# An encoder layer's MLP beginning in another order, finishing work in steps of 512 columns, and four side steps per block in the last gate group

## The chip, the cores and the metric

The kernel runs on one core of one Trainium2 chip. The metric is the device time of one execution in microseconds (us). Each time given for a kernel is the median of several runs; the profile is of one execution, taken by the hardware profiler. The engines are TensorE (PE, matrix products; PEld is its loading of weights), VectorE (DVE), ScalarE (ACT), GpSimd (POOL) and SyncE (SP), which here issues the DMA transfers.

## The reference

One layer of an encoder on 1536 tokens of width 1024 (512 tokens of one request and 1024 of another), in float32:

```python
def _layer(h, p_i, ...):
    a = _rmsnorm(h, norm_mix_g)
    z = a @ w_in                                   # q, k, v, and the pooling channels u
    o_attn = _attention(q, k, v, q_norm_g, k_norm_g)
    o_pool = _pool_mixer(u, w_pool, pool_scale)
    h = h + jnp.concatenate([o_attn, o_pool], axis=-1) @ w_out
    m = _rmsnorm(h, norm_mlp_g)
    h = h + jnp.square(jax.nn.relu(m @ w_up)) @ w_down       # hidden width 4096
    gate = jax.nn.sigmoid(_rmsnorm(h, norm_ple_g) @ w_ple_gate)
    h = h + gate * (p_i @ w_ple_proj)
    return h
# and a last _rmsnorm(h, final_norm_g)
```

## The kernel before

**Layout and chunks.** Everything is kept transposed: the 1024 features lie on partitions, tokens are columns. The tokens are three chunks c = 0, 1, 2 of 512 columns; the residual h of a chunk is four tiles `hT[c][a]` of 128 x 2 x 512 (256 features each, two halves of 512 columns in a row; 512 KB). Each float32 product is made of three products of a high and a low half (`three`): the high half is a cast by ACT to a shorter format, the low half the difference, made by POOL or DVE.

**Stages, by the trace:** the input projection to about 194 us, attention and the pooling mixer with the output projection (`heads_out`, which adds into h) to 579, the MLP to 1613, and the gate and the last norm to the end.

**The MLP** runs over 48 `Pair`s: 16 for each chunk, each of two blocks of 128 of the 4096 hidden units. A pair makes the hidden values by seven products in Strassen's manner, in the order 1, 6, 2, 5, 7, 3, 4, into four banks (x, y, z, q; tiles px, py, pz, pq). Its weights `w..._i` are sums of the loaded `wur` (L793 to L804, DVE), cast by ACT (L786) and with a low half by POOL (L787). The factors on the other side, `mo`, are the seven combinations of the normalised h; `make_m(c)` computes them chunk by chunk in advance, stores them to DRAM (L636) and has them loaded again. It also computes w, the mean square of h (the norm's factor), as `acc[:, 1]` (tile sqm), and stores it to `w_d` (L647). The pair ends in a chain: DVE adds bank q (L870 for product 7, L880 for product 4), ACT makes relu and two squares (L875 to L877 and L881 to L883), DVE the low half of r (L886). The next pair's products are mixed with `down(a)` of this one: 12 products of r and the down weights wd, added to h by DVE (L837). The order on TensorE is px(1), `down(0)`, py(6), px(2), `down(1)`, pz(5), pq(7), `down(2)`, pz(3), pq(4), `down(3)`.

The norm's factor is not applied to m. Instead h is multiplied by w before the MLP's sums are added to it (`raise_h`, L662, eight steps on DVE), and at the chunk's end by its inverse (`invert`, L670, and L1138).

**Side work.** After each of the seven products the loop calls `after(i)`: one step of `feeding` (the weights of pairs ahead; the next `load_up()` is issued in its step 3), one step of `splits` (the down weights, L816, L817), one of `raising`, and `step()`, one step of a list of generators called `chores`: `spill`, `invert`, `make_m`, and `finishing(c)`, which in the MLP of chunk c + 1 scales the finished h of chunk c, stores it to `hl_d`, squares it on ACT (L1142) and for c = 0 makes the gate's input (L1126). Chores run one behind another, so a longer one delays those behind it.

**What sets the order.** PE, ACT, DVE and POOL run their instructions in the order in which the program issues them; SP's transfers are put in order by a scheduler, and each waits for the eighth before it on the ring of semaphores. Buffers come from 49 slots in turn (`slot`): a new tile takes the slot of an old one and waits for the last reader of it, which can be a DMA that stores the old tile.

The last part is `gate`, called for (c, o, w) = (0, 0, 512), (1, 0, 512), (2, 0, 256), (2, 256, 256); each has eight blocks d of 24 matmuls (tile pg), and `hooks` lists the k at which a chore's step is taken in a block.

## Time and profile before

| | before |
|---|---|
| median of 3 runs | 1814.47 us (1813.41 to 1815.92) |
| profiled execution | 1813.31 us, span 1811.5 |
| PE busy | 1759.7 us, 97% |
| DVE busy | 1260.0 us, 70% |
| ACT busy | 939.7 us, 52% |
| POOL busy | 1053.7 us, 58% |
| DMA | 256.84 MB, mean 142 GB/s |

Rows of a timeline give the start, the duration, the engine, the line, the operation, the tile written and those read, and the count of instructions in the row; in square brackets how long the engine stood idle before it and what released it. "PE pd L49 <- DVE r L886: 10.6, 11, 1.8" in a list of waits says that PE, at its product into pd, waited for DVE's r of line 886 10.6 us in all, 11 times, at most 1.8 us. "issue" stands where the profile shows no release. SPq is the queue from which SP issues transfers. Line 49 is the helper of all matrix products, line 56 that of all loads. Numbers of chunks and pairs are left out of the names of tiles in the profile.

### The profile page before, as it was taken

To read this page: it belongs to the slowest core of one execution; us is meant where nothing else is said; L and a number is where in the kernel's file an instruction comes from. 1 tells how busy PE (TensorE), PEld (TensorE's weight loads), DVE (VectorE), ACT (ScalarE), POOL (GpSimd) and SP (SyncE) were. 2 spreads that over 40 slices of the span, in tenths; PEclk is the share of its full clock that TensorE was granted. 3 is DMA by queue.
4 is the path that set the end of the run, shared out by engine and by line. 5 is a ranking of instruction groups with operands and counts; after the bars stand their busy time and mean duration, and the time that the engine had idled before them with its cause. 6 is when DMAs were issued, how large, how long until landed. Compare 5 with 4: busy or idle time off the path is not lost.

```text
span 1811.5 us, 28604 instructions
## 1 busy us (share of the span) xinstructions
PE 1759.7 (97%) x10540; PEld 1537.1 (85%) x10540; DVE 1260.0 (70%) x1843; ACT 939.7 (52%) x1854; POOL 1053.7 (58%) x923
## 2 busy tenths in 40 slices
PE   9999899999999799999999999999999999999997
PEld 7888777888868798988888889889898999888887
DVE  5677865888894677865568877876776556665655
ACT  6434455768794455655445545554455444443332
POOL 3474774535674567676656776785577666543121
PEclk9999999999999899999999999999999999999998
DMA  6333545120519335343364442556443323272102
GB/s 248 114 123 105 216 165 185 36 94 13 206 46 367 139 122 198 121 177 100 136 265 157 163 151 96 195 185 235 179 157 100 110 94 99 89 262 70 59 12 82
DMA packets 83883, 256.84 MB, mean 142 GB/s; under 512 B 9888, under 2 KB 16416, under 8 KB 83744
## 3 DMA queue, kind: packets, MB, share of 16 engines
q1 hardware_dynamic: 83744, 255.02, 39.7%
q8 instruction: 83, 1.36, 0.3%
q14 instruction: 56, 0.46, 0.1%
HBM read 195.74 MB, written 59.24 MB: 141 GB/s over the span
## 4 chain that ended last, share of the span: by engine, by line
PE 78%; DVE 7%; ACT 5%; DMA 3%; issue 3%; POOL 1%; POOLq 0%; DVEq 0%; ACTq 0%; SPq 0%
PE pd L49 25%; PE z L49 7%; PE px L49 6%; PE pz L49 6%; PE pq L49 6%; PE pg L49 6%; PE py L49 4%; PE pp L49 3%; PE o L49 3%; PE tp L53 3%; PE po L49 3%; PE S L49 3%; PE pj L49 1%; DMA wur<-in_w_up_dram 1%; DVE r L886 1%
## 5 line engine op out<-in xcount | busy, mean ns | idle before, releaser
L49 PE MATMUL pd<-r,wd 128*128 128x512 f32 x2304 | 568.5, 395 | 10.8 <-DVE r L886 10.6
L49 PEld LDWEIGHTS pd<-r,wd 128*128 128x128 f32 x2304 | 419.5, 188 | 100.3 <-DVE r L886 16.1
L787 POOL TENSOR_TENSOR w<-ws,w 128x512 fp32r<-128x512 f32 x192 | 272.5, 1423 | 217.9 <-ACT w L786 206.8
L787 POOL TENSOR_TENSOR w<-wur,w 128x512 fp32r<-128x512 f32 x144 | 212.8, 1489 | 135.4 <-ACT w L786 134.4
L837 DVE TENSOR_TENSOR h<-pd,h 128x1024 f32<-128x1024 f32 x192 | 233.5, 1216 | 76.6 <-PE pd L49 76.5
L786 ACT CAST w<-ws 128x512 fp32r<-128x512 f32 x192 | 118.5, 617 | 271.1 <-DVE ws L795 241.1
L461 POOL TENSOR_SCALAR pr<-pr,rr 128x512 f32<-128x512 f32 x160 | 111.2, 705 | 134.7 <-DVE rr L456 66.8
L49 PE MATMUL z<-w,x 128*128 128x512 f32 (+1 forms) x864 | 175.7, 359 | 0.9 <-DVE w L160 0.5
L49 PEld LDWEIGHTS pz<-mo,w 128*128 128x128 f32 x1152 | 150.7, 190 | 19.3 <-issue 11.2
L49 PEld LDWEIGHTS z<-w,x 128*128 128x128 f32 x864 | 142.9, 189 | 28.0 <-ACT w L159 2.1
L49 PE MATMUL pz<-mo,w 128*128 128x256 f32 x1152 | 153.6, 283 | 10.2 <-issue 10.2
L817 DVE TENSOR_TENSOR wd<-wdr,wd 128x512 fp32r<-128x512 f32 x96 | 102.8, 1071 | 83.1 <-ACT wd L816 76.6
L49 PE MATMUL pq<-mo,w 128*128 128x256 f32 x1152 | 153.7, 283 | 1.0 <-issue 1.0
L49 PE MATMUL px<-mo,w 128*128 128x256 f32 x1152 | 152.2, 281 | 0.0
L49 PEld LDWEIGHTS px<-mo,w 128*128 128x128 f32 x1152 | 146.5, 189 | 4.0
L49 PEld LDWEIGHTS pq<-mo,w 128*128 128x128 f32 x1152 | 144.7, 191 | 1.4 <-issue 1.3
L49 PE MATMUL pg<-hg,wg 128*128 128x512 f32 (+1 forms) x768 | 141.0, 338 | 0.2
L472 ACT CAST pt<-tp 128x512 fp32r<-128x512 f32 x160 | 88.0, 591 | 88.5 <-PE tp L53 86.8
L49 PEld LDWEIGHTS pg<-hg,wg 128*128 128x128 f32 x768 | 118.6, 188 | 17.8 <-DVE hg L1128 1.0
L817 POOL TENSOR_TENSOR wd<-wdr,wd 128x512 fp32r<-128x512 f32 x96 | 131.8, 1373 | 2.6 <-DMA w_d<-sqm 2.6
L886 DVE TENSOR_TENSOR r<-c,r 128x512 fp32r<-128x512 f32 x96 | 74.7, 783 | 74.1 <-ACT c L883 46.2
L473 DVE TENSOR_TENSOR pt<-tp,pt 128x512 fp32r<-128x512 f32 x160 | 104.0, 684 | 31.4 <-ACT pt L472 31.1
(195 smaller groups left out, 3036.2 us busy)
## 6 DMA issues: line engine op xcount, KB each, us to landing
wur<-in_w_up_dram SPq DMA_DIRECT2D x96, 512.0 KB, 4.2
wdr<-in_w_down_dram SPq DMA_DIRECT2D x96, 512.0 KB, 4.4
mo_d<-mm SPq DMA_DIRECT2D x84, 256.0 KB, 2.3
mo<-mo_d SPq DMA_DIRECT2D x42, 512.0 KB, 7.7
h_d<-h SPq DMA_DIRECT2D x16, 512.0 KB, 3.0
h<-h_d SPq DMA_DIRECT2D x16, 512.0 KB, 9.9
xn<-in_xn_dram SPq DMA_DIRECT2D x12, 512.0 KB, 6.4
qs_d<-qs SPq DMA_DIRECT2D x12, 512.0 KB, 3.0
```

Of the source, the lines that this page charges most:

```text
L49: last_pe[0] = nc.tensor.matmul(*a, **k).ins
L53: last_pe[0] = nc.tensor.transpose(*a, **k).ins
L461: gp.tensor_scalar(p, p, rr, 1.0, op0=ALU.mult, op1=ALU.mult)
L472: sc.copy(self.pt[kt][:, 0], tp)
L473: ve.tensor_tensor(self.pt[kt][:, 1], tp, as32(self.pt[kt][:, 0]), op=ALU.subtract)
L786: sc.copy(t[:, 0], x)
L787: gp.tensor_tensor(t[:, 1], x, as32(t[:, 0]), op=ALU.subtract)
L817: (gp, ve)[i].tensor_tensor(lo, self.dr[i][:, h], as32(hi), op=ALU.subtract)
L837: ve.tensor_tensor(h, pd.rearrange("p (a b) -> p a b", a=2), h, op=ALU.add)
L886: ve.tensor_tensor(self.r[i][:, 1], x, as32(self.r[i][:, 0]), op=ALU.subtract)
```

## The change

- `make_m(0)` keeps w of chunk 0 in its tile (`ws[0] = acc[:, 1]`): it isn't stored to `w_d` and loaded again; `load_ms` is called for chunks 1 and 2 alone.
- The h of chunk 2 is stored to `h_d` right in `heads_out`, tile by tile at odd d, where before `spill(2)` did it after 16 steps of waiting. The chores behind it (`invert(0)`, `make_m(1)`) are then the next in the list.
- The loads of pair 1's up weights are issued ahead of those of h of chunk 0, not in `feeding`'s step 3 of pair 0.
- Ahead of the MLP five steps of `feeding` are taken instead of four; in pair 0 no step of it follows product 4, `splits` runs after products 5, 7, 3 and 4 alone, and `raise_h` takes two steps after 2, 5, 7 and 3 (none after 1 and 6). From pair 1 on the steps stand as before.
- `finishing` squares a tile in halves of 512 columns with a step for each, and makes the two halves of the gate's input in two steps: 38 steps for chunk 0 instead of 26, 22 for chunk 1 instead of 18.
- In the gate groups with o > 0, the last one, `hooks` are (1, 3, 6) in every block: with the `step()` ahead of the block four steps, where there were two.

```diff
@@ -644,7 +644,10 @@
         for i in range(2):
             pe.matmul(bc, ones_sb, sh[:, i], start=i == 0, stop=i == 1)
         ve.tensor_scalar(acc[:, 1], bc, 1.0 / D, EPS, op0=ALU.mult, op1=ALU.add)
-        sy.dma_start(w_d[c], acc[:, 1])
+        if c:
+            sy.dma_start(w_d[c], acc[:, 1])
+        else:
+            ws[0] = acc[:, 1]
 
     def load_mo(c, i):
         MO[c, i] = [slot([P, 4, HF], F32R, f"mo{c}_{i}{j}") for j in range(2)]
@@ -703,7 +706,6 @@
     away = set()
 
     def spill(c):
-        yield from wait(16 if c == 2 else 0)
         for a in range(4):
             sy.dma_start(h_d[c][a], hT[c][a])
         away.add(c)
@@ -753,7 +755,10 @@
                     for i, (w_, x_) in enumerate(three(ws, [x[:, k, :] for x in cat[p]])):
                         pe.matmul(po, w_, x_, start=k == 0 and i == 0, stop=k == 3 and i == 2)
                 ve.tensor_tensor(h, po, h, op=ALU.add)
-                if d == KD - 1 and p % 2:
+                if p == 5:
+                    if d % 2:
+                        sy.dma_start(h_d[c][d // 2], hT[c][d // 2])
+                elif d == KD - 1 and p % 2:
                     chores.append(spill(c))
                     if c == 0:
                         chores.append(make_m(0, gp, gp))
@@ -893,7 +898,7 @@
 
         for n, pr in enumerate(pairs):
             for i, _ in enumerate(pr.feed()):
-                if i == 3 and n + 1 < len(pairs):
+                if i == 3 and 0 < n < len(pairs) - 1:
                     pairs[n + 1].load_up()
                 yield
     feeding = stream()
@@ -1067,12 +1072,13 @@
 
     pairs[0].load_down()
     load_mo(0, ORDER[5]), load_mo(0, ORDER[6])
+    pairs[1].load_up()
     for a in range(4):
         load_h(0, a, h_d[0][a])
     while fill:
         fill.popleft()()
         step(2)
-        if len(fill) % 2 == 0 and len(fill) < 8:
+        if len(fill) % 2 == 0 and len(fill) < 12:
             next(feeding)
     ps_free()
     acc_free()
@@ -1139,10 +1145,12 @@
                 yield
             sy.dma_start(hl_d[c][a], h)
             sq = slot([P, 2, CH], F32, f"sqg{c}{a}") if a else acc
-            sc.activation(sq, h, AF.Square)
-            if c == 0:
-                gate_in(0, a, True)
-            yield
+            for e in range(2):
+                sc.activation(sq[:, e], h[:, e], AF.Square)
+                yield
+            for e in range(2) if c == 0 else ():
+                gate_in(0, a, True, (e,))
+                yield
             for e in range(2) if a else ():
                 gp.tensor_tensor(acc[:, e], acc[:, e], sq[:, e], op=ALU.add)
                 yield
@@ -1184,7 +1192,7 @@
             if c:
                 for a in range(4):
                     load_h(c, a, h_d[c][a])
-            load_ms(c)
+                load_ms(c)
             raising = raise_h(c)
         if g == 1:
             chores.append(invert(c))
@@ -1202,9 +1210,11 @@
                 pairs[n + 1].load_down()
 
         def after(i):
-            next(feeding, None)
-            next(splits, None)
-            if raising:
+            if n or i != 4:
+                next(feeding, None)
+            if n or i in (5, 7, 3, 4):
+                next(splits, None)
+            for _ in range(0 if not raising else 1 if c else 0 if i in (1, 6) else 2):
                 next(raising, None)
             if g == NG - 1 and c < 2:
                 load_mo(c + 1, i)
@@ -1244,7 +1254,7 @@
                 pe.matmul(pj, w_, x_, start=k == 0 and i == 0, stop=k == 1 and i == 2)
         step()
         pg = ps("g", f"pg{c}{o}{d}")[:, :w]
-        hooks = () if c == 1 and d == KD - 1 or c == 2 and o == 0 else (2, 5) if c == 1 else (3,)
+        hooks = (1, 3, 6) if o else () if c == 1 and d == KD - 1 or c == 2 and o == 0 else (2, 5) if c == 1 else (3,)
         if c == 0 and d % 2 == 0 and d < KD - 2:
             for j in range(2):
                 load_g(d // 2 + 1, j)
```

SP's transfers at the MLP's beginning, before (h00 to h03 are chunk 0's tiles, h20 to h23 chunk 2's, wur0_10 and wur0_11 the up weights of pair 1, h_d2 the spilled h of chunk 2):

```order
L56 DMA mo0_41_6354<-mo_d0_41_275 128x1024
L56 DMA h00_6357<-h_d0_0_304 128x1024
L56 DMA h01_6359<-h_d0_1_305 128x1024
L56 DMA h02_6361<-h_d0_2_306 128x1024
L56 DMA h03_6363<-h_d0_3_307 128x1024
L647 DMA w_d0_259<-sqm0_4189 128x512
L708 DMA h_d2_0_312<-h20_5526 128x1024
L708 DMA h_d2_1_313<-h21_5528 128x1024
L708 DMA h_d2_2_314<-h22_5530 128x1024
L56 DMA wur0_10_6531<-in_w_up_dram 128x1024
L56 DMA wur0_11_6532<-in_w_up_dram 128x1024
L56 DMA w0_6556<-w_d0_259 128x512
```

and now:

```order
L56 DMA mo0_41_6354<-mo_d0_41_275 128x1024
L56 DMA wur0_10_6357<-in_w_up_dram 128x1024
L56 DMA wur0_11_6358<-in_w_up_dram 128x1024
L56 DMA h00_6361<-h_d0_0_304 128x1024
L56 DMA h01_6363<-h_d0_1_305 128x1024
L56 DMA h02_6365<-h_d0_2_306 128x1024
L56 DMA h03_6367<-h_d0_3_307 128x1024
L760 DMA h_d2_0_312<-h20_5526 128x1024
L760 DMA h_d2_1_313<-h21_5528 128x1024
L760 DMA h_d2_2_314<-h22_5530 128x1024
L760 DMA h_d2_3_315<-h23_5532 128x1024
L56 DMA wdr0_10_6622<-in_w_down_dram 128x1024
```

The store and load of w are gone, the up weights stand ahead of h, and all four spills of chunk 2's h stand together behind the loads of h.

DVE's row in pair 0, from the add of product 5 on, before (c0_0 is the pair's hidden values, r0_00 and r0_01 its result, wd0 its down weights):

```order
L866 TENSOR_TENSOR u0_0_6558<-pz0_0_6630,u0_0_6558 128x256
L793 TENSOR_TENSOR ws0_10_6644<-wur0_11_6532 128x512
L817 TENSOR_TENSOR wd0_011_6583<-wdr0_01_6346,wd0_010_6582 128x512
L662 TENSOR_TENSOR h01_6359<-h01_6359,w0_6556 128x512
L870 TENSOR_TENSOR c0_0_6559<-pq0_0_6653,u0_0_6558 128x256
L795 TENSOR_TENSOR ws0_10_6644<-ws0_10_6644,wur0_10_6531 128x512
L662 TENSOR_TENSOR h02_6361<-h02_6361,w0_6556 128x512
L874 TENSOR_TENSOR c0_0_6559<-pz0_0_6630,u0_0_6558 128x256
L662 TENSOR_TENSOR h02_6361<-h02_6361,w0_6556 128x512
L880 TENSOR_TENSOR c0_0_6559<-pq0_0_6653,u0_0_6558 128x256
L801 TENSOR_TENSOR ws0_11_6645<-wur0_10_6531,wur0_11_6532 128x512
L662 TENSOR_TENSOR h03_6363<-h03_6363,w0_6556 128x512
```

and now:

```order
L871 TENSOR_TENSOR u0_0_6563<-pz0_0_6626,u0_0_6563 128x256
L800 TENSOR_TENSOR ws0_10_6614<-ws0_10_6614,wur0_10_6357 128x512
L665 TENSOR_TENSOR h01_6363<-h01_6363,sqm0_4189 128x512 x2
L875 TENSOR_TENSOR c0_0_6564<-pq0_0_6652,u0_0_6563 128x256
L665 TENSOR_TENSOR h02_6365<-h02_6365,sqm0_4189 128x512 x2
L879 TENSOR_TENSOR c0_0_6564<-pz0_0_6626,u0_0_6563 128x256
L806 TENSOR_TENSOR ws0_11_6615<-wur0_10_6357,wur0_11_6358 128x512
L822 TENSOR_TENSOR wd0_011_6647<-wdr0_01_6346,wd0_010_6646 128x512
L665 TENSOR_TENSOR h03_6367<-h03_6367,sqm0_4189 128x512 x2
L885 TENSOR_TENSOR c0_0_6564<-pq0_0_6652,u0_0_6563 128x256
L822 TENSOR_TENSOR wd0_011_6647<-wdr0_01_6346,wd0_010_6646 128x512
L891 TENSOR_TENSOR r0_00_6565<-c0_0_6564,r0_00_6565 128x512
```

The multiplications of h (L662, now L665) come in twos, and both differences of the down weights (L817, now L822) stand between product 3's add and r. The tile c0_0 now takes the slot of h20 and the weight w0_1_1 of pair 1 that of h21, so L875 on DVE and L866 on ACT wait for the store of h20, and the cast of w0_1_1 (L791) on ACT for that of h21. In ACT's row the casts of pair 0's down weights moved with them, before:

```order
L786 CAST w0_0_3_6601<-ws0_01_6431 128x512
L816 CAST wd0_000_6580<-wdr0_00_6345 128x512
L861 ACTIVATE c0_0_6559<-px0_0_6562 128x256
L786 CAST w0_0_4_6620<-wur0_01_6098 128x512
L816 CAST wd0_010_6582<-wdr0_01_6346 128x512
L786 CAST w0_1_1_6646<-wur0_10_6531 128x512
L816 CAST wd0_010_6582<-wdr0_01_6346 128x512
L786 CAST w0_1_6_6668<-ws0_10_6644 128x512
L875 ACTIVATE c0_0_6559<-c0_0_6559 128x256
L876 ACTIVATE r0_00_6560<-c0_0_6559 128x512
L877 ACTIVATE c0_0_6559<-c0_0_6559 128x512
L786 CAST w0_1_2_6688<-wur0_10_6531 128x512
```

and now:

```order
L791 CAST w0_1_1_6616<-wur0_10_6357 128x512
L791 CAST w0_1_6_6641<-ws0_10_6614 128x512
L821 CAST wd0_000_6644<-wdr0_00_6345 128x512
L791 CAST w0_1_2_6666<-wur0_10_6357 128x512
L821 CAST wd0_000_6644<-wdr0_00_6345 128x512
L880 ACTIVATE c0_0_6564<-c0_0_6564 128x256
L881 ACTIVATE r0_00_6565<-c0_0_6564 128x512
L882 ACTIVATE c0_0_6564<-c0_0_6564 128x512
L791 CAST w0_1_5_6689<-ws0_10_6614 128x512
L821 CAST wd0_010_6646<-wdr0_01_6346 128x512
L886 ACTIVATE c0_0_6564<-c0_0_6564 128x512
L887 ACTIVATE r0_01_6566<-c0_0_6564 128x512
```

The second block's casts (wd0_010) now stand on either side of r0_01's chain.

ACT's row in chunk 1, at the work on chunk 0's tile h01 (sqg01 its squares, hg01 the gate's input), before:

```order
L786 CAST w1_3_1_10605<-wur1_30_10461 128x512
L816 CAST wd1_210_10511<-wdr1_21_10360 128x512
L786 CAST w1_3_6_10627<-ws1_30_10603 128x512
L1142 ACTIVATE sqg01_10631<-h01_6359 128x1024
L1126 ACTIVATE hg01_0_10633<-h01_6359,gple_sb_230 128x512 x2
L875 ACTIVATE c1_2_10488<-c1_2_10488 128x256
L876 ACTIVATE r1_20_10489<-c1_2_10488 128x512
L877 ACTIVATE c1_2_10488<-c1_2_10488 128x512
```

and now:

```order
L1149 ACTIVATE sqg01_10730<-h01_6363 128x512
L791 CAST w1_3_3_10760<-ws1_31_10597 128x512
L821 CAST wd1_300_10723<-wdr1_30_10578 128x512
L1149 ACTIVATE sqg01_10730<-h01_6363 128x512
L866 ACTIVATE c1_3_10702<-px1_3_10705 128x256
L791 CAST w1_3_4_10779<-wur1_31_10459 128x512
L821 CAST wd1_310_10725<-wdr1_31_10579 128x512
L1132 ACTIVATE hg01_0_10784<-h01_6363,gple_sb_230 128x512
L791 CAST w1_4_1_10821<-wur1_40_10680 128x512
L821 CAST wd1_310_10725<-wdr1_31_10579 128x512
L1132 ACTIVATE hg01_0_10784<-h01_6363,gple_sb_230 128x512
L791 CAST w1_4_6_10843<-ws1_40_10819 128x512
```

The square of 1024 columns and both halves of the gate's input stood in a row ahead of a relu (L875); now single halves stand apart, with casts between them.

SP's row at the change from chunk 1 to chunk 2, now (w_d2 is chunk 2's w; before, the store stood 19 rows ahead of wur2_10, right behind wur1_151):

```order
L56 DMA mo2_31_13599<-mo_d2_31_301 128x1024
L648 DMA w_d2_261<-sqm2_11936 128x512
L56 DMA wur2_10_13627<-in_w_up_dram 128x1024
L56 DMA wur2_11_13628<-in_w_up_dram 128x1024
L56 DMA mo2_40_13631<-mo_d2_40_302 128x1024
L56 DMA mo2_41_13632<-mo_d2_41_303 128x1024
L56 DMA h20_13651<-h_d2_0_312 128x1024
L56 DMA h21_13653<-h_d2_1_313 128x1024
L56 DMA h22_13655<-h_d2_2_314 128x1024
L56 DMA h23_13657<-h_d2_3_315 128x1024
L56 DMA w2_13659<-w_d2_261 128x512
```

The 256 KB store stands ahead of the up weights of pair 1 and of the load of h and w.

## The prediction

> **What bounds the kernel now.** I read the page first, then TensorE's waits, then the stretches where those waits lie, engine by engine. The page gives TensorE (PE) nearly the whole span:

> ```profile
> span 1811.5 us, 28604 instructions
> PE 1759.7 (97%) x10540; PEld 1537.1 (85%) x10540; DVE 1260.0 (70%) x1843; ACT 939.7 (52%) x1854; POOL 1053.7 (58%) x923
> ```

> So only PE's idle time (1811.5 - 1759.7 = 51.8 us) and its half-clock time can be won; a step saved on another engine counts where PE waits for it. TensorE's waits name two kinds:

> ```profile
> PE pd L49 <- DVE r L886: 10.6, 11, 1.8
> PE pz L49 <- issue: 10.2, 3, 9.2
> ```

> In the first `down` waits for the low half of r, the last product of a pair's chain ACT, ACT, ACT, DVE; in the second one wait of 9.2 us has no releaser named. TensorE's timeline puts that one at the MLP's beginning:

> ```profile
> 583.28 1.59 PE L49 MATMUL pz<-mo,w 128*128 128x256 f32 x12
> 584.71 1.57 PE L49 MATMUL pq<-mo,w 128*128 128x256 f32 x12
> 595.48 2.90 PE L49 MATMUL pz<-mo,w 128*128 128x256 f32 x12 [9.20 <-issue]
> ...
> 602.18 0.40 PE L49 MATMUL pd<-r,wd 128*128 128x512 f32 x1
> 604.34 0.96 PE L49 MATMUL pd<-r,wd 128*128 128x512 f32 x3 [1.77 <-DVE r L886]
> 607.99 1.60 PE L49 MATMUL py<-mo,w 128*128 128x256 f32 x12
> ```

> DVE's timeline tells why. Product 3 adds into bank z, which L866 must have read; L866 stands behind h's multiplication, which waited for w to come back from DRAM:

> ```profile
> 592.22 0.69 DVE L662 TENSOR_TENSOR h<-h,w 128x512 f32<-128x512 f32 x1 [11.38 <-DMA w<-w_d]
> ...
> 594.96 0.42 DVE L866 TENSOR_TENSOR u<-pz,u 128x256 f32<-128x256 f32 x1
> ...
> 601.91 1.77 DVE L662 TENSOR_TENSOR h<-h,w 128x512 f32<-128x512 f32 x1
> 603.61 2.38 DVE L886 TENSOR_TENSOR r<-c,r 128x512 fp32r<-128x512 f32 x2
> ```

> The windows of that stretch (columns: window, length, then PE, PEld, DVE, ACT and POOL busy, granted clock, DMA share, GB/s) show full queues and afterwards a halved clock:

> ```profile
> 586.20:595.40 9.20, 0.08 (x1) 0.00 (x0) 3.18 (x7) 1.14 (x2) 5.44 (x5) 0.74 1.02 413
> 595.40:598.40 3.00, 2.92 (x14) 2.95 (x15) 3.00 (x6) 0.25 (x1) 0.00 (x0) 0.50 0.30 122
> 598.40:602.60 4.20, 4.18 (x25) 3.85 (x24) 3.90 (x6) 3.69 (x7) 2.47 (x2) 0.71 0.23 27
> ```

> At 413 GB/s a 512 KB transfer takes 524288 / 413000 = 1.27 us. After the stall two products (24 matmuls) took from 595.48 to 600.74 = 5.26 us, where an undisturbed one takes 1.43 (pz at 583.28 to pq at 584.71): 5.26 - 2.86 = 2.4 us lost to the clock.

> **The beginning, part by part.** w no longer goes through DRAM, so that wait is gone. What is late next? The transfers ahead of the new order are those of SP's rows: mo4, two wur, four h, four spilled h_d2. To place them I need one landing of before: ACT's first cast of pair 1 was released by its wur.

> ```profile
> 590.35 0.62 ACT L786 CAST w<-wur 128x512 fp32r<-128x512 f32 x1 [5.46 <-DMA wur<-in_w_up_dram]
> ...
> 599.53 0.63 ACT L876 ACTIVATE r<-c 128x512 fp32r<-128x512 f32 x1
> 600.19 0.63 ACT L877 ACTIVATE c<-c 128x512 f32<-128x512 f32 x1
> 600.73 0.60 ACT L786 CAST w<-wur 128x512 fp32r<-128x512 f32 x1
> ```

> In before's order eight and a half transfers of 512 KB (four h, the 256 KB of w_d, three h_d, this wur) lie between mo4 and that moment, so mo4 landed at about 590.3 - 8.5 x 1.27 = 579.5. In after's order the same pace gives wur 580.8 and 582.0, h 583.3 to 587.1, h_d2 tile 0 at 588.4, tile 1 at 589.6. Two of these are new waits: c of pair 0 now takes the buffer that h's tile 0 of chunk 2 left, so DVE's L875 and ACT's relu L866 wait for the spill of tile 0; the weight w of pair 1's product 1 takes tile 1's buffer, so ACT's cast L791 waits for 589.6. Behind L875 on DVE stand the whole rest of the pair's chain; behind L866 and the cast on ACT the same.

> PE then runs product 3 from 586.1 without the stall, idles from 587.5 until L875 has read bank q (588.9), runs product 4 to 590.3, idles until POOL has made the low half of the weight. POOL's timeline has its price:

> ```profile
> 591.04 1.26 POOL L787 TENSOR_TENSOR w<-wur,w 128x512 fp32r<-128x512 f32 x1 [0.67 <-ACT w L786]
> ```

> 589.6 + 0.6 + 1.3 = 591.5, so px of pair 1 ends at 592.9, and PE needs r. ACT has from 589.6: three casts of w and two of wd (pitch 0.54, by the rows above), relu, two squares (0.66, 0.54), one more cast of w and one of wd: about 5.3 us, to 595.0. Then DVE's wd difference and h's last two multiplications stand ahead of L885: 3 x 0.6 = 1.8 us alone, 3 x 1.75 = 5.2 beside POOL (1.77 against 0.69 for L662 above). Then ACT relu, two squares, a cast (2.4 us) and DVE's wd difference and first L886 (1.2 to 3): r's low half at 601.2 if DVE is never held, 604.1 if it is. In before the same mix of casts, POOL differences and h multiplications was held, so I take 603.7. From there 2.9 us of `down` and the half clock's 2.4 us (PE is idle from 592.9 for over 8 us, nearly as long as the 9.2 that halved it before) put py of pair 1 at 609.0, against 607.99: **+1.0 us**. Ends: 601.2 with no clock loss, 604.1 - 608 = -3.9; 604.1 with POOL a difference (1.3) later, +2.5.

> [...]

> [...]

> The fifth feed step is work taken from pair 0; from pair 1 on the distance is as before, so chunk 0's interior counts 0 (±0.5).

> **End of a chunk's MLP (finishing).** The time from a pair to the next is read where DVE adds q of product 4:

> ```profile
> 963.41 0.42 DVE L880 TENSOR_TENSOR c<-pq,u 128x256 f32<-128x256 f32 x1 [0.40 <-PE pq L49]
> 984.48 0.42 DVE L880 TENSOR_TENSOR c<-pq,u 128x256 f32<-128x256 f32 x1 [0.88 <-PE pq L49]
> 1006.62 0.42 DVE L880 TENSOR_TENSOR c<-pq,u 128x256 f32<-128x256 f32 x1
> 1029.69 0.42 DVE L880 TENSOR_TENSOR c<-pq,u 128x256 f32<-128x256 f32 x1
> 1052.76 0.42 DVE L880 TENSOR_TENSOR c<-pq,u 128x256 f32<-128x256 f32 x1 [0.38 <-PE pq L49]
> ```

> An undisturbed pair takes 21.07; the next three take 22.14, 23.07, 23.07: 5.07 us lost. ACT's rows in the second show the cause:

> ```profile
> 1005.73 1.05 ACT L1142 ACTIVATE sqg<-h 128x1024 f32<-128x1024 f32 x1
> 1006.69 1.32 ACT L1126 ACTIVATE hg<-h,gple_sb 128x512 fp32r<-128x512 f32 x2
> 1007.92 0.40 ACT L875 ACTIVATE c<-c 128x256 f32<-128x256 f32 x1
> ```

> 2.2 us of side work stand ahead of the relu, which could have run at 1006.6. After has a step of at most 0.6 there, spread over four; the pairs' own slack took less than 2.2 - 2.0 = 0.2 of it, so a half step (0.5) can still show in a pair: **-4.8** (ends -5.1, all of it; -3.5, 0.5 left in each of three pairs). With a step for each half the work on chunk 0's end takes twelve steps more, and chunk 2's preparation, which runs behind it in the same list, comes later. Its casts then meet relu chains in other pairs; before they cost 1.5 once:

> ```profile
> PE pd L49 <- DVE r L886: 1.5, 1, 1.5
> ```

> (TensorE's waits from 1130 to 1165.) After, by the order, one pair has two 0.7 us ACTIVATEs ahead of its relu where that pair had two casts: **-0.2**, between -1.5 (no such meeting) and +1.5 (two).

> In chunk 2 the Square stands between the fourth product's add and its relu:

> ```profile
> 1354.34 0.42 DVE L880 TENSOR_TENSOR c<-pq,u 128x256 f32<-128x256 f32 x1
> 1376.61 0.43 DVE L880 TENSOR_TENSOR c<-pq,u 128x256 f32<-128x256 f32 x1
> ...
> 1356.63 1.06 ACT L1142 ACTIVATE sqg<-h 128x1024 f32<-128x1024 f32 x1
> ```

> 22.27 - 21.07 = 1.2 lost; in halves and in other steps **-1.2** (-0.5 where one half, 0.5, still stands there; -1.4).

> **The seam from chunk 1 to 2.** The later preparation moves the 256 KB store of w into the one stretch where SP's transfers fall behind: w's load was issued at 1270.69 and landed ten us later.

> ```profile
> 1261.92 0.81 SPq L56 DMA_DIRECT2D wur<-in_w_up_dram  x2
> ...
> 1270.69 0.32 SPq L56 DMA_DIRECT2D w<-w_d  x1
> ...
> 1267.58 0.42 DVE L880 TENSOR_TENSOR c<-pq,u 128x256 f32<-128x256 f32 x1 [1.01 <-PE pq L49]
> ...
> 1280.34 1.14 DVE L662 TENSOR_TENSOR h<-h,w 128x512 f32<-128x512 f32 x1 [7.16 <-DMA w<-w_d]
> ```

> A transfer of half the size ahead makes w 0.64 later: **+0.65**, 0.3 if part of it is covered, 1.3 if the store also holds a ring's place.

> **The last gate group.** Two more steps per block empty the side work sooner, but the end follows the last block's own chain:

> ```profile
> 1799.19 0.42 DVE L1268 TENSOR_TENSOR s<-pg,bcs 128x256 f32<-128x256 f32 x1 [0.56 <-PE pg L49]
> ...
> 1801.54 0.83 PE L49 MATMUL ssf<-ones_sb,s 128*128 128x1 f32 x6 [1.16 <-ACT s L1272]
> ```

> Its first operation waits for PE, so it isn't late by side work: **0** (±0.3: PE's small sums stand earlier among its matmuls, and may wait a few tenths for POOL).

> **Sum:** +1.0 + 0 - 4.8 - 0.2 + 0.65 - 1.2 + 0 = -4.55. The profiled execution took 1813.31 (span 1811.5), so its counterpart comes to 1808.8; the median of the runs, 1814.47, lies 1.16 higher: **1810.0 us**. What a measurement can tell from no change is 0.2%, 3.6 us: the line lies at 1810.8.

> **Rivals.**
> [...]
> *C, the steps don't remove the chunk's losses.* Twice as many small pieces meet the relus in more pairs, or POOL's differences get held by DVE's more scattered work; then half or less of the 5.07 and 1.2 comes back. -2.5 and -0.3 in place of -4.8 and -1.2, with +1.0, +0.65 and +1.0 of casts: 1814.3. For it: relu chains that are late by single casts exist (the 1.5 above). Against it: pairs with a cast alone run at 21.07.
> *D, slower: the seam.* The store of w stands ahead of SP's load of wur at 1261.92 and can't leave before DVE has computed w, in after just behind the pair's last q (DVE does the row's L880 there at 1267.6). If SP stands still these 5.8 us long enough for the transfers in flight to run out, w's load lands 5.8 later, DVE's multiplication and the banks behind it too, and PE idles that long and then loses the clock's 2.4: +8.2, in all 1814.5 + 3.6 = 1818. It decides if the backlog at 1261.9 is under 5.8 us; against it speaks w's load, which took ten us to land, so a backlog of about eight.

> **How the numbers follow.** Main case 0.63 (1810.0, own range 1806 to 1813: the ends of the terms, not all at once); B 0.11; C 0.20; D 0.06. The main case lies under 1810.8 in 65 of 100, 0.41. Faster: 0.41 + 0.11 + 0.02 of C = 0.54. Same: 0.22 + 0.16 of C = 0.38. Slower: 0.06 + 0.02 of C = 0.08. The range 1805 to 1816 leaves out B and D, 0.17.

> **What would show it.** Beginning: DVE L875 released by a DMA h_d2 at about 588.5, PE's largest gap 7 to 10 us long but behind px of pair 1, a clock of 0.5 behind it, py at 606 to 610. Chunk 1: the three pairs at 21.1 to 21.6 instead of 22.1 to 23.1, TensorE's wait for r (10.6) down to about 6. Chunk 2: one pair less at 22.3. Seam: DVE's wait for w 0.6 longer. I am wrong if the pairs of chunk 1 stay above 22, or if h_d2 lands before 586 or after 591.

## The result, and the profile after

The changed kernel takes 1833.45 us (median; 1832.98 to 1836.97), before 1814.57: a ratio of 1.0108, 95% interval 1.0096 to 1.012. It is slower by 19 us, where 1810.0 was forecast. The profiled execution has a span of 1831.5 us, 20.0 more than before's 1811.5.

The page of the changed kernel, first lines, and then TensorE's longest waits in it:

```profile
span 1831.5 us, 28583 instructions
PE 1768.5 (97%) x10540; PEld 1541.7 (84%) x10540; DVE 1254.4 (68%) x1843; ACT 940.6 (51%) x1862; POOL 1049.2 (57%) x923
```

```profile
PE pd L49 <- DVE r L891: 23.2, 12, 10.0
PE pd L49 <- DVE h L842: 5.4, 1, 5.4
```

PE is idle 63.0 us instead of 51.8; its busy time grew by 8.8 with the same 10540 products, as products at a halved clock take longer: eleven products into pd took 2.69 us at 1188.68, at the clock 1.00, and 4.63 at 1194.94, with the clock at 0.50 from 1195.02 to 1198.43. The 10.2 us of before's wait at pz are gone, and the wait for r grew from 10.6 to 23.2; its longest, 10.0 us, is the beginning's.

Where the 20 us arose is read from the times at which DVE adds product 4 of a pair (the rows L880, now L885), as in the prediction. A table of the differences between such rows, from the two traces, and of the kernels run afterwards (us; "0.1" is pair 1 of chunk 0):

| stretch | before | changed | finishing only | 12 idle steps | idle steps behind the factor | b6 |
|---|---|---|---|---|---|---|
| first px to py of pair 0.1 | 28.98 | 29.49 | | | | 19.39 |
| 0.1 to 0.15 | 296.60 | 297.64 | 296.64 | 296.63 | 296.68 | 296.20 |
| 1.1 to 1.6 | 111.79 | 108.51 | 108.63 | 110.51 | 111.84 | 109.29 |
| 1.6 to 1.9 | 63.64 | 71.84 | 72.34 | 72.26 | 63.44 | 63.53 |
| 1.9 to 1.15 | 128.74 | 135.35 | 134.07 | 134.19 | 134.12 | 128.51 |
| 1.15 to 2.0 | 23.96 | 29.73 | 30.24 | 30.31 | 30.02 | 21.95 |
| 2.0 to 2.15 | 318.18 | 318.53 | 318.35 | 318.58 | 318.48 | 317.66 |

The gain of the finer steps is there (-3.3 in 1.1 to 1.6). What came on top are three losses behind it: 8.2, 6.6 and 5.8 us. Of the first two numbers, 1.3 us are one and the same work: TensorE's ten small products for the gate norm's factor (ssg, 0.81 us from its start to the next product's, and bcg, 0.46) left the stretch 1.1 to 1.6 for 1.6 to 1.9. Before, and then changed:

```profile
1060.96 0.95 PE L49 MATMUL ssg<-ones_sb,sqg 128*128 128x1 f32 x8
```

```profile
1094.41 0.95 PE L49 MATMUL ssg<-ones_sb,sqg 128*128 128x1 f32 x8
```

Without that move the gain is 2.0 us and the first loss 6.9.

**The first, pair 1.7.** DVE's timeline, and then POOL's, in the changed kernel:

```profile
1094.61 0.42 DVE L885 TENSOR_TENSOR c<-pq,u 128x256 f32<-128x256 f32 x1 [0.99 <-PE pq L49]
1094.95 0.68 DVE L806 TENSOR_TENSOR ws<-wur,wur 128x512 f32<-128x512 f32 x1
1095.55 0.15 DVE L537 TENSOR_SCALAR rsg<-ssg 128x4 f32<-128x4 f32 x1
1101.06 2.51 DVE L552 TENSOR_TENSOR dgg<-id_sb,rhg 128x512 fp32r<-128x512 f32 x2 [5.36 <-POOL rhg L548]
1103.50 2.35 DVE L891 TENSOR_TENSOR r<-c,r 128x512 fp32r<-128x512 f32 x2
```

```profile
1096.04 1.30 POOL L792 TENSOR_TENSOR w<-wur,w 128x512 fp32r<-128x512 f32 x1 [3.08 <-ACT w L791]
1098.47 1.28 POOL L792 TENSOR_TENSOR w<-ws,w 128x512 fp32r<-128x512 f32 x1 [1.13 <-ACT w L791]
1099.72 1.02 POOL L538 TENSOR_TENSOR rsg<-rsg,mhalf 128x4 f32<-128x4 f32 x1
```

At the end of `finishing(0)` one step makes the gate norm's factor: DVE scales the sums (L537), POOL takes the root (L538, L548), DVE spreads it (L552). Twelve steps later than before, this step falls behind product 4, so L552 stands ahead of r (L891) in DVE's row. POOL's part stands behind two weight differences that wait for ACT, DVE stands still 5.36 us for it, and r comes at 1103.5 though its inputs were there from 1097.9 (ACT's last square ran at 1097.26). In before the same step fell behind product 6 of pair 1.6, DVE's row there:

```profile
1061.23 0.42 DVE L858 TENSOR_TENSOR u<-py,u 128x256 f32<-128x256 f32 x1 [0.29 <-PE py L49]
1061.95 0.16 DVE L537 TENSOR_SCALAR rsg<-ssg 128x4 f32<-128x4 f32 x1 [0.29 <-PE ssg L49]
1065.20 2.54 DVE L552 TENSOR_TENSOR dgg<-id_sb,rhg 128x512 fp32r<-128x512 f32 x2 [3.09 <-POOL rhg L548]
```

There DVE waits 3.09 us too, but the r that the running `down` products need (pair 1.5's) was done at 1057.3, and PE doesn't wait. The windows of the changed kernel (columns as in the prediction) show the idle time and the clock behind it:

```profile
1099.90:1105.30 5.40, 0.01 (x2) 0.00 (x1) 4.14 (x4) 1.22 (x3) 4.62 (x5) 0.77 0.49 181
1105.30:1112.00 6.70, 6.70 (x29) 5.71 (x30) 3.88 (x5) 1.14 (x2) 2.53 (x2) 0.67 0.44 149
```

**The second and third, chunk 2's preparation.** `make_m(2)` runs behind `finishing(0)` in the same list, so it comes later as well. In pair 1.11 DVE's sum of weights L806, which stands ahead of r, waits 3.62 us for a store of m, and at the change to chunk 2 SP's transfers are late. DVE's timeline at both places, then SP's:

```profile
1193.59 0.69 DVE L806 TENSOR_TENSOR ws<-wur,wur 128x512 f32<-128x512 f32 x1 [3.62 <-DMA mo_d<-mm]
1194.20 2.37 DVE L891 TENSOR_TENSOR r<-c,r 128x512 fp32r<-128x512 f32 x2
...
1279.75 0.69 DVE L646 TENSOR_SCALAR sqm<-w 128x512 f32<-128x512 f32 x1
1281.16 0.42 DVE L885 TENSOR_TENSOR c<-pq,u 128x256 f32<-128x256 f32 x1 [0.72 <-PE pq L49]
...
1300.15 0.69 DVE L665 TENSOR_TENSOR h<-h,w 128x512 f32<-128x512 f32 x1 [13.84 <-DMA w<-w_d]
```

```profile
1256.31 7.87 SPq L636 DMA_DIRECT2D mo_d<-mm  x5
...
1280.47 0.32 SPq L648 DMA_DIRECT2D w_d<-sqm  x1
1281.04 1.59 SPq L56 DMA_DIRECT2D wur<-in_w_up_dram  x2
...
1290.57 0.32 SPq L56 DMA_DIRECT2D w<-w_d  x1
```

Measured from the last pair's add of product 4, wur was issued 0.12 us ahead (1281.04 against 1281.16), before 5.66 ahead (1261.92 against 1267.58). The loads of mo ahead of it, counted the same way, were already 4.0 to 4.7 us late behind the stores of m (SP is at them until 1264). The rest comes with w's store: SP issued nothing for 1.7 us until DVE's L646 was done. w's load was issued 9.4 us behind that add (3.1 before), and DVE waits 13.84 us for it instead of 7.16.

**The beginning's chain** went as forecast. TensorE's timeline in the changed kernel, and DVE's and ACT's rows that carry the new waits:

```profile
589.53 1.67 PE L49 MATMUL pq<-mo,w 128*128 128x256 f32 x12 [1.26 <-ACT c L866]
...
592.74 1.45 PE L49 MATMUL px<-mo,w 128*128 128x256 f32 x10 [1.24 <-POOL w L792]
...
604.54 4.57 PE L49 MATMUL pd<-r,wd 128*128 128x512 f32 x11 [9.98 <-DVE r L891]
608.95 1.60 PE L49 MATMUL py<-mo,w 128*128 128x256 f32 x12
```

```profile
589.00 0.42 DVE L875 TENSOR_TENSOR c<-pq,u 128x256 f32<-128x256 f32 x1 [0.68 <-DMA h_d<-h]
```

```profile
590.33 0.62 ACT L791 CAST w<-wur 128x512 fp32r<-128x512 f32 x1 [0.98 <-DMA h_d<-h]
```

### The profile page after: what moved, and what is told of

It reads as the page before. It is cut to its first block, busy times and chain, and to the rows that moved or that the text cites. A ratio compares the mean times of both kernels' runs of the same rounds, so it can differ in the third digit from the quotient of the medians.

```text
span 1831.5 us, 28583 instructions
## 1 busy us (share of the span) xinstructions
PE 1768.5 (97%) x10540; PEld 1541.7 (84%) x10540; DVE 1254.4 (68%) x1843; ACT 940.6 (51%) x1862; POOL 1049.2 (57%) x923
## 5 line engine op out<-in xcount | busy, mean ns | idle before, releaser
L49 PE MATMUL pd<-r,wd 128*128 128x512 f32 x2304 | 577.2, 399 | 29.1 <-DVE r L891 23.2
L49 PEld LDWEIGHTS pd<-r,wd 128*128 128x128 f32 x2304 | 424.2, 190 | 122.1 <-DVE r L891 31.3
L791 ACT CAST w<-ws 128x512 fp32r<-128x512 f32 x192 | 118.4, 617 | 266.6 <-DVE ws L800 227.5
L49 PE MATMUL z<-w,x 128*128 128x512 f32 (+1 forms) x864 | 175.4, 359 | 0.7 <-DVE w L160 0.5
L822 DVE TENSOR_TENSOR wd<-wdr,wd 128x512 fp32r<-128x512 f32 x96 | 102.1, 1064 | 103.8 <-ACT wd L821 93.7
L49 PEld LDWEIGHTS z<-w,x 128*128 128x128 f32 x864 | 142.9, 189 | 27.6 <-ACT w L159 2.4
L49 PEld LDWEIGHTS pz<-mo,w 128*128 128x128 f32 x1152 | 149.8, 189 | 9.4 <-issue 0.9
L49 PE MATMUL pq<-mo,w 128*128 128x256 f32 x1152 | 152.7, 282 | 3.0 <-DVE c L875 1.3
L49 PE MATMUL px<-mo,w 128*128 128x256 f32 x1152 | 152.7, 282 | 1.2 <-POOL w L792 1.2
L49 PE MATMUL pz<-mo,w 128*128 128x256 f32 x1152 | 152.4, 281 | 0.5 <-issue 0.5
L49 PEld LDWEIGHTS px<-mo,w 128*128 128x128 f32 x1152 | 146.7, 189 | 5.5 <-POOL w L792 1.4
L49 PEld LDWEIGHTS pq<-mo,w 128*128 128x128 f32 x1152 | 143.5, 189 | 3.8 <-issue 2.3
L49 PE MATMUL pg<-hg,wg 128*128 128x512 f32 (+1 forms) x768 | 141.7, 339 | 0.2
L49 PEld LDWEIGHTS pg<-hg,wg 128*128 128x128 f32 x768 | 119.0, 188 | 18.0 <-DVE hg L1134 1.0
L822 POOL TENSOR_TENSOR wd<-wdr,wd 128x512 fp32r<-128x512 f32 x96 | 130.3, 1358 | 0.0
L891 DVE TENSOR_TENSOR r<-c,r 128x512 fp32r<-128x512 f32 x96 | 81.3, 855 | 63.0 <-ACT c L888 47.3
```

Of the source, the lines that this page charges most:

```text
L49: last_pe[0] = nc.tensor.matmul(*a, **k).ins
L791: sc.copy(t[:, 0], x)
L822: (gp, ve)[i].tensor_tensor(lo, self.dr[i][:, h], as32(hi), op=ALU.subtract)
L891: ve.tensor_tensor(self.r[i][:, 1], x, as32(self.r[i][:, 0]), op=ALU.subtract)
```

## The experiments

Theory of lateness: the finer finishing is harmless as such, but its twelve extra steps move what stands behind it in the list. Rival: the many small pieces collide with the pairs' chains. Each kernel differs from the one named by the diff alone, in which "..." marks lines left out; ratios are to runs of before made with them. Times are medians, stretches those of the one profiled execution.

**e1: the beginning alone.** The changed kernel with before's `finishing` and `hooks`.

```diff
-            for e in range(2):
-                sc.activation(sq[:, e], h[:, e], AF.Square)
-                yield
-            for e in range(2) if c == 0 else ():
-                gate_in(0, a, True, (e,))
-                yield
+            sc.activation(sq, h, AF.Square)
+            if c == 0:
+                gate_in(0, a, True)
+            yield
...
-        hooks = (1, 3, 6) if o else () if c == 1 and ...
+        hooks = () if c == 1 and ...
```

> The change without its finishing steps and without its last gate hooks (both as before): only the MLP's beginning is new. By the sum of the two traces the beginning costs 0.9 us at pair 0.1 and another 1.0 in chunk 0's interior, so 1816.5 (+2). Rival: the stores of chunk 2's h and the earlier chores also bring the losses of chunks 1 and 2; then 1825 or more.

Measured: 1817.55, ratio 1.0015 (1.0006 to 1.0024). The stretches 1.1 to 1.6, 1.6 to 1.9 and 1.9 to 1.15 take 111.77, 63.51 and 128.32 as before; 0.1 to 0.15 takes 297.62 (+1.0), the first px to py of pair 0.1 29.79 (+0.8). The beginning costs about two us, twice the forecast's one. The interior's 1.0 us are two waits of PE for r (1.1 us in all; before has 0.2). Only 1.15 to 2.0 differs from before's too, 25.00 (+1.0); in x below, with the same beginning, it is 23.91, so the beginning has no part in the three losses.

**e2: the finer finishing alone.** Before with the first part of this diff the other way round (its six lines with - in place of the four with +).

> Before with nothing but the finishing in halves (a step each). Theory: nearly all of the loss comes with it, +17.5 us (20 less 2.2 for the beginning and 0.3 for the tail), 1832; the wait of 5.4 us for r in pair 1.7 and the late load of w at the seam appear. Rival: half of the loss needs the beginning's change too, 1823.

Measured: 1832.48, ratio 1.0097 (1.008 to 1.0114). All three losses are in the table's column. So this edit alone costs 17 us.

**e3: twelve idle steps and nothing finer.** Before, and

```diff
-        yield from wait(6)
+        yield from wait(6 if c else 18)
         yield from spread_g(c, acc)
```

> Before with its whole squares and undivided gate input, but twelve idle steps ahead of the norm's factor in finishing(0). Theory of lateness: the steps' number does the harm, by putting the factor's chain ahead of r in pair 1.7 and chunk 2's preparation twelve steps later: +8.2 +6.6 +5.8 = +20.6, 1835, with the three slow pairs of chunk 1 (22.1 to 23.1) as before. Rival, collisions of the many small pieces: no pieces, so within 2 us of before, 1814 to 1817.

Measured: 1835.11, ratio 1.011 (1.0095 to 1.0125). No piece is smaller and no operation is added, yet the three losses stand in the table: 8.6, 5.5 and 6.4 us, where the changed kernel has 8.2, 6.6 and 5.8. That excludes collisions of small pieces as their cause. (The 1.1 us between 5.5 and 6.6 go with a halving of the clock that the changed kernel has there, 3.41 us at 0.50; e4 below, which loses 5.4 there, has its clock at 1.00 from 1177 to 1198, around the same pair; see the last section.) TensorE's and DVE's waits in it carry the same two signs:

```profile
PE pd L49 <- DVE r L886: 17.6, 13, 5.4
PE pd L49 <- DVE h L837: 6.0, 1, 6.0
...
DVE h L662 <- DMA w<-w_d: 32.4, 3, 14.4
```

**e4: the idle steps behind the factor.** Before, and

```diff
         yield from wait(6)
         yield from spread_g(c, acc)
+        yield from wait(0 if c else 12)
```

> Before with the twelve idle steps behind the norm's factor and ahead of chunk 2's preparation. Theory of lateness, in two parts: the factor's chain stands as before, so no long wait in pair 1.7 (-8.2 against the last kernel), but the preparation is late: +6.6 +5.8 = +12.4, 1827. If the long wait of 1.7 was due to the preparation and not to the factor's place, it appears here too and the time is 1835. Collisions: 1814 to 1817.

Measured: 1827.5, ratio 1.0063 (1.0048 to 1.0078). 1.6 to 1.9 takes 63.44, the first loss is gone; the other two stay (134.12, 30.02). TensorE's waits here have no 5.4:

```profile
PE pd L49 <- DVE r L886: 12.5, 13, 1.6
PE pd L49 <- DVE h L837: 5.8, 1, 5.8
```

**e5: the factor four steps earlier,** in the changed kernel.

```diff
-        yield from wait(6)
+        yield from wait(6 if c else 2)
         yield from spread_g(c, acc)
+        yield from wait(0 if c else 4)
```

> The changed kernel, with four of the six idle steps ahead of the norm's factor in finishing(0) moved behind it: the factor's chain falls four steps earlier, behind product 2 of a pair instead of product 4, chunk 2's preparation begins where it did. Theory: the 8.2 us around pair 1.7 go and nothing else, 1825. Rival: that loss belongs to the pair (transfers, weights) or moves to another row; then 1831 to 1834.

Measured: 1829.12, ratio 1.0075 (1.0059 to 1.009), where 1825 was expected. 1.6 to 1.9 fell from 71.84 to 65.27, so 6.6 of the 8.2 us went and 1.6 stayed. Of these, 1.3 are the factor's own ten products, which now run in this stretch (pair 1.6 to 1.7 takes 22.52, before 21.14); PE's waits for r from 1070 to 1135 are 0.3 us in all. So behind product 2 the factor costs next to nothing but its products, and the expected 1825 had counted them as loss. Another 1.3 us lie ahead of pair 0.1, which this execution reached later; the rest of the miss stays open.

**e6: w of chunk 2 kept in its tile,** on e4.

```diff
-        sy.dma_start(w_d[c], acc[:, 1])
+        if c == 2:
+            ws[2] = acc[:, 1]
+        else:
+            sy.dma_start(w_d[c], acc[:, 1])
...
-            load_ms(c)
+            if c < 2:
+                load_ms(c)
```

> The kernel with twelve idle steps behind the factor (1827.5), and w of chunk 2 kept in its tile as the change does for chunk 0: no store and load of it at the change to chunk 2. If the 6.1 us there are the wait for w, pair 2.0 comes to about 25 instead of 30.0 after the one ahead and the time to 1822; the losses of 1.11 to 1.15 stay. If the transfers of m's factors and weights behind the late stores hold TensorE, too, no more than 1 to 2 us come back, 1826.

Measured: 1822.87, ratio 1.0043 (1.0028 to 1.0058). 1.15 to 2.0 fell from 30.02 to 25.90: 4.1 of the third loss's 6.1 us are the wait for w. 1.9 to 1.15 took 137.03 in this execution, 2.9 more than in e4; it was the slowest of the four (1825.65), at a mean granted clock of 0.991 (e4's profiled execution 0.993). What is late next at the change of chunks, DVE's timeline says:

```profile
1292.52 0.69 DVE L665 TENSOR_TENSOR h<-h,sqm 128x512 f32<-128x512 f32 x1 [10.02 <-DMA h<-h_d]
```

**m1: halves in the old number of steps.** Before, with each tile's pieces regrouped: first multiplication; second and first square; second square; each half's gate input with POOL's sum of that half; the low parts. 26 and 18 steps, as before.

```diff
+            ve.tensor_tensor(h[:, 0], h[:, 0], ws[c], op=ALU.mult)
+            yield
+            ve.tensor_tensor(h[:, 1], h[:, 1], ws[c], op=ALU.mult)
+            sc.activation(sq[:, 0], h[:, 0], AF.Square)
+            yield
+            sy.dma_start(hl_d[c][a], h)
+            sc.activation(sq[:, 1], h[:, 1], AF.Square)
+            yield
+            for e in range(2):
+                if c == 0:
+                    gate_in(0, a, True, (e,))
+                if a:
+                    gp.tensor_tensor(acc[:, e], acc[:, e], sq[:, e], op=ALU.add)
...
```

> Before with squares and gate input in halves of 512 columns, but put into the steps that there were (26 and 18): the second multiplication's step takes the first square, POOL's sums go with the gate input. Theory of lateness: the gain without the loss, the pairs 1.2 to 1.4 at 21.1 to 21.5 (-3.4 to -4.9), 0 to -1.2 in chunk 2: 1810 (-4.5). Collisions: the small pieces cost where the large ones did, 1813 to 1815.

Measured: 1813.29, ratio 0.9989 (0.998 to 0.9998), a small gain, about half of that expected. 1.1 to 1.6 takes 109.29 (-2.5), 1.6 to 1.15 is as before. TensorE's waits from 980 to 1060 fell to

```profile
PE pd L49 <- DVE r L886: 1.6, 3, 0.6
```

from 3.7, and ACT's timeline shows why they did not go: one half still stands ahead of the second relu.

```profile
1029.71 0.72 ACT L1126 ACTIVATE hg<-h,gple_sb 128x512 fp32r<-128x512 f32 x1
1030.34 0.62 ACT L881 ACTIVATE c<-c 128x512 f32<-128x512 f32 x1
```

**x: the changed kernel with m1's steps.** Its `finishing` replaced by m1's.

> The changed kernel with the halves put into before's number of steps (26 and 18). If the parts add up: before's time, +2 for the beginning, -2.5 for the halves, +0.3 for the tail, 1814 to 1815.5, 18 us less than the changed kernel. If the late chunk work needs something else of the change too, it stays above 1820.

Measured: 1812.72, ratio 0.9987 (0.9978 to 0.9996): the whole slowdown is gone, 20.7 us, by regrouping the same operations into fewer steps. It came out 1.3 us under the expected range, by no more than runs of one kernel differ.

**The hooks alone.** Before with the changed kernel's line `hooks`.

> Before with nothing but four side steps per block in the last gate group. By the two traces the tail grew by 0.3 us: 1814.5 to 1815.5, no difference that can be measured. Rival: the tail's larger wait (2.28 us ahead of the last small sums instead of 0.85 and 1.16) is this part's and costs 1 us.

Measured: 1814.68, ratio 0.9999 (0.999 to 1.0009). No difference, as forecast; the larger wait ahead of the last small sums (2.3 us once) takes the place of two smaller ones.

**e7: the stores of chunk 2's h between the loads.** e1, with

```diff
-    pairs[1].load_up()
-    for a in range(4):
-        load_h(0, a, h_d[0][a])
     while fill:
         fill.popleft()()
+        if len(fill) == 6:
+            pairs[1].load_up()
+        if len(fill) in (6, 4, 2, 0):
+            load_h(0, 3 - len(fill) // 2, h_d[0][3 - len(fill) // 2])
...
-            if n or i in (5, 7, 3, 4):
-                next(splits, None)
-            for _ in range(0 if not raising else 1 if c else 0 if i in (1, 6) else 2):
+            next(splits, None)
+            for _ in range(0 if not raising else 1 if c else 0 if i in (1, 6, 2) else 1):
```

> Before's finishing and hooks with the new beginning, but the loads of pair 1's weights and of h are issued between the stores of chunk 2's h, the down weights are cast as early as in the kernel before, and h is multiplied in single steps, the last four behind r. By the landings (1.27 us each from 579.5) the stores of tiles 0 and 1 land at 580.8 and 585.9, so no chain waits for them; r at 592, py of pair 1 at 595 instead of 608: 13 us less than before and 1 more in the interior, 1803. Rival: the chain of r is bound by ACT's and DVE's own work, a gap of 5 us or more stays and the clock is halved: 1809 to 1812.

Measured: 1810.29, ratio 0.9976 (0.9966 to 0.9985). py of pair 0.1 comes 22.32 after the first px (28.98 before), 6.7 us gained instead of 13. The rival was right: no transfer is waited for in c or the cast, but DVE's row holds the chain, with operations of 1.4 to 1.75 us ahead of L875; a gap of 4.62 us stays, and the clock is halved for 3.4 us behind it (0.53 from 594.80 to 597.50, 0.82 to 600.00):

```profile
591.07 1.70 DVE L822 TENSOR_TENSOR wd<-wdr,wd 128x512 fp32r<-128x512 f32 x1 [1.21 <-ACT wd L821]
592.70 1.75 DVE L665 TENSOR_TENSOR h<-h,sqm 128x512 f32<-128x512 f32 x1
594.37 0.41 DVE L875 TENSOR_TENSOR c<-pq,u 128x256 f32<-128x256 f32 x1
```

**b5: a bare chain.** e7 and m1 together, and in pair 0 all down-weight casts by product 2, h multiplied only behind r and in pair 1; eight idle steps ahead of `invert(0)`.

```diff
-            next(splits, None)
-            for _ in range(0 if not raising else 1 if c else 0 if i in (1, 6, 2) else 1):
+            for _ in range(1 if n or i != 6 else 2):
+                next(splits, None)
+            for _ in range(1 if raising and n else 0):
...
-        raising = None
+        raising = raising if n == 1 else None
...
+            chores.append(wait(0 if c else 8))
             chores.append(invert(c))
...
-        for _ in raising or ():
-            pass
+        for k, _ in enumerate(raising or ()):
+            if n == 0 and k:
+                break
```

> The halves in the old steps, and the beginning once more: stores of chunk 2's h between the loads, all four casts of the down weights ahead of the next pair's weights, h multiplied behind r and in pair 1, chores in pair 1 delayed by eight steps as before. Nothing then stands between the products and r but the chain itself: no gap of TensorE over 3 us, the clock stays at 1.0, py of pair 1 at 596 to 598 (608 before). With the halves' 2.5: 1800 to 1803. If POOL's differences (1.3 to 1.75 each) bind instead, a gap of 4 to 5 us stays and the time is 1805 to 1808.

Measured: 1802.12, ratio 0.9927 (0.9912 to 0.9942). py of pair 0.1 comes 18.84 after the first px, 10.1 us sooner than before; the largest gap there is 2.23 us and the clock stays at 1.00. Chunk 0's interior takes 296.23, so its loss of 1.0 is gone too; which of the edits did that was not separated.

**b6: b5 with e6's edit.**

> The same with w of chunk 2 kept in its tile. Pair 2.0 took 23.9 to 24.6 after the one ahead, 2.9 to 3.5 more than a pair; where the wait for w causes part of it, 0.5 to 2 us less than the kernel ahead. If the products of m's factors bind there, no difference.

Measured: 1799.74, ratio 0.9912 (0.9896 to 0.9929), 34 us less than the changed kernel and 15.6 less than before. 1.15 to 2.0 takes 21.95 (b5 24.02). TensorE's timeline at the beginning, to be laid beside the one above:

```profile
589.36 2.20 PE L49 MATMUL pz<-mo,w 128*128 128x256 f32 x12 [2.23 <-issue]
591.36 2.61 PE L49 MATMUL pq<-mo,w 128*128 128x256 f32 x12
593.81 1.57 PE L49 MATMUL px<-mo,w 128*128 128x256 f32 x12
...
597.32 2.12 PE L49 MATMUL pd<-r,wd 128*128 128x512 f32 x8 [0.94 <-DVE r L891]
599.27 1.59 PE L49 MATMUL py<-mo,w 128*128 128x256 f32 x12
```

The two gaps of 2.23 and 0.94 us are what is left of 9.20, 1.77 and 0.74 before.

## Why the prediction was wrong

*The beginning* (+1.0, own ends -3.9 and +2.5) was right in place and size: L875 at 589.0 by the store of h (588.4 forecast), the cast at 590.3 (589.6), r at 604.5 (603.7), py at 608.95 (609.0). That py fits to 0.05 us is luck: r came 0.8 later, and the products and the clock behind it took 4.4 instead of 5.3. The end for a DVE that is held, 604.1, also doesn't follow from its own terms (595.0 + 5.2 + 2.4 + 3 = 605.6). The 1.0 us more in chunk 0's interior was counted as 0 ± 0.5.

*The chance for B* (0.11, the beginning's stall gone altogether) was the author's estimate. In e7 no chain waits for a store and py comes 6.7 us sooner, but a gap of 4.62 us stays with the halved clock behind it.

*Finishing's gain* (-4.8) was mis-sized: the stretch 1.1 to 1.6 gained 3.3. Of that, e3 shows that 1.3 (111.79 to 110.51) come from the factor's own products leaving the stretch, so the pieces alone gave about 2, and m1 with everything else in place 2.5. The three slow pairs take 21.14, 22.93 and 22.39: two stay above 22, the prediction's own sign of being wrong, and rival C's -2.5 is nearer than -4.8. In chunk 2 the pair of 22.27 did fall to 21.37, but the -1.2 was read from it alone, though the pair ahead had taken only 20.65; the pairs around it took the gain back (20.65 to 21.13, 22.43 to 22.86), and 2.0 to 2.15 takes 0.35 more than before.

*The step that failed* is the one on what the twelve steps push back. It spoke of chunk 2's casts alone (-0.2, at most +1.5) and named nothing else that stands in the list. Two things were left out or mis-sized there. The gate norm's factor, a chain from DVE to POOL and back inside one step, has no term in the sum; it cost 6.9 us (8.2 in its stretch, less the 1.3 of its products, which before has elsewhere), shown by e3 (it comes with idle steps) and e4 and e5 (it goes when the factor stands elsewhere). And the preparation's lateness, priced by one cast's collision, cost 6.6, of which e4 shows 5.4 without any finer piece. The rest goes with one halving of the clock, 3.41 us at 0.50 in pair 1.11: e4 has its clock at 1.00 there (1177 to 1198) and loses 5.4; finishing only and e3 lose 5.3 and 5.5. The waits for stores and the casts ahead of relus, which make up the 5.4, were not separated.

*The seam* (+0.65) was priced as 256 KB of extra transfer. Rival D had what came of it, w late, PE idle (5.42 us at its wait for h) and the clock at 0.50 behind it (1300.83 to 1307.65), and nearly its size (8.2; measured 5.8), but with a chance of 0.06. Its reason was a small part of it: SP stood still for w's store for 1.7 us, not 5.8, and the loads of mo were already 4.0 to 4.7 us late behind the stores of m. The argument against it, a backlog of eight us at 1261.9, was taken from before's queue, which those stores had not delayed. e6 confirms w as 4.1 us of it.

*The hooks* (0) were right.

So 19.3 us of loss (6.9 + 6.6 + 5.8) stood against terms of -0.2 + 0.65, and the range's upper end, built from collisions, could not hold it.

## What to carry to other kernels

Where side work is a list with one step per hook, splitting a step also delays everything behind it in the list. Cost that first: find each chain between engines that lies further down, and look in the new order at what stands behind its waiting instruction, above all a main chain's last operation on the same engine. Splitting within the old number of steps (two small pieces on different engines in one step) keeps the gain without the move; here that is worth 20.7 us. And a wait removed at a stage's start pays only as far as the chain behind it is bare: the changed beginning gained nothing, e7's 6.7 us, b5's 10.

## What the runs showed of the hardware that was not expected

Gaps of TensorE much shorter than the beginning's (9.20 us in before, 9.98 in the changed kernel) already had the halved clock behind them, and of two gaps of one length one had it and one had not. The changed kernel has a gap of 1.90 us in pair 1.11 (ending at 1194.94); b6 and b5 have the same gap of 2.23 us at the beginning. Behind the first two the clock is at 0.50 for 3.41 us, behind b5's it stays at 1.00. The windows of the changed kernel, of b6 and of b5:

```profile
1191.60:1195.02 3.42, 1.52 (x13) 1.21 (x11) 1.43 (x3) 2.90 (x6) 2.18 (x3) 1.00 1.04 402
1195.02:1198.43 3.41, 3.33 (x7) 2.20 (x8) 3.41 (x3) 1.14 (x2) 2.50 (x3) 0.50 1.03 399
```

```profile
586.83:590.24 3.41, 1.18 (x10) 1.00 (x9) 3.41 (x4) 0.00 (x0) 3.23 (x2) 1.00 1.03 418
590.24:593.66 3.42, 3.42 (x18) 3.42 (x17) 2.28 (x4) 2.62 (x5) 2.32 (x2) 0.50 1.03 419
```

```profile
585.85:589.26 3.41, 2.91 (x25) 2.70 (x23) 3.14 (x3) 1.55 (x4) 3.41 (x3) 1.00 1.03 418
589.26:592.68 3.42, 1.67 (x13) 1.53 (x13) 3.32 (x4) 0.40 (x1) 2.44 (x2) 1.00 1.03 419
592.68:596.09 3.41, 3.31 (x25) 2.99 (x25) 3.31 (x4) 3.29 (x7) 3.12 (x3) 1.00 1.04 418
```

From these numbers follows an estimate for this kernel: a gap under 1.75 us (b5's 0.51 of 3.413) in otherwise busy products leaves the clock alone, one over twice 1.83 us halves it, and between them it depends on where the gap falls, as with b6's and b5's 2.23. By the same estimate each period at 0.50 costs up to 1.7 us of products, half its length, on top of the gap. The second loss agrees with it: e4, whose longest wait of PE for r is 1.6 us, has its clock at 1.00 around pair 1.11, the changed kernel 0.50 behind its 1.90.
